# First attention of a transformer layer: value units over three buffers, head outputs with their own, three key buffers, and the first pair's units ahead of one query unit

## The chip, the cores and the metric

The kernel runs on one core of one Trainium2 chip. The metric is the device time of one execution in microseconds (us); lower is better. The core has a matmul engine (TensorE, PE in the profile; PEld is its weight load), a vector engine (DVE), a scalar engine (ACT) and GpSimd (POOL). SyncE (SP) does no arithmetic: it issues all the transfers, one after the other, and an issue that has to wait holds up those behind it. Each engine works through its own list of instructions in the order in which they stand; semaphores make one wait for another.

## What is computed

One layer on 1024 tokens of width 1024, all in float32: a feed-forward block, a token mixer, a second feed-forward block, and norms between them. The token mixer is what the change touches:

```python
h = rmsnorm(x, mix_norm)
proj = h @ w_in                                   # q, k, v of both attentions, gates
# first ("differential") attention, 8 heads, two score maps c = 0, 1 for each head
q, k = rope(q_da), rope(k_da)
p = softmax(causal(q[h, c] @ k[h, c].T / 8))
a = p[c=0] - lam * p[c=1]
y_da[h] = rmsnorm(a @ v_da[h], head_gain[h]) * (1 - lam_init)
# second attention (NSA): 16 query heads over compressed, selected and windowed keys
y_ns = nsa(q_ns, compressed k/v, k_slc, v_slc, k_win, v_win, gates)
out = (sigmoid(g_a) * (y_da @ w_proj_da) + sigmoid(g_b) * (y_ns @ w_proj_nsa)) @ w_out
```

## The kernel before

Every float32 product is made of three matmuls on a high and a low half of each operand: `mm3` writes `hi*hi`, `lo*hi` and `hi*lo` (lines 49 to 51). `split` (line 86) makes the halves: ACT copies the high half, DVE subtracts it for the low half (line 82).

The mixer's projections are cut into *units*, each with one or two weight tiles of 128 columns, and each in two halves `tb` of 512 tokens. Eight times three matmuls (24, on the tensor `gm`) fill one PSUM bank. A *rope unit* (`rope_pair`) has two weight tiles: DVE multiplies `gm` by cosine and sine into the tiles `m13` and `m42`, POOL joins them, `split` writes `rh` and `rl`, and two or three stores take these to DRAM (`sq` queries, `sk` keys of the first attention, `sqn` NSA queries). A *value unit* (`v_da_unit`) has one: DVE scales `gm` into `vt` (a tile with tag `m13`, line 568), PE transposes it (line 571), `split` writes `vh` and `vl` (tags `rh`, `rl`), and two stores take them to `sv`. The pool `mp` that holds `m13`, `m42`, `rh` and `rl` has one buffer for each tag, 4 KB on each partition, so whoever takes a tag next waits until the stores from it have landed.

Before the first attention (`prelim`) come the NSA key, value and query units; each of the four NSA query units `u` is a rope unit with `cmp_block`, scores against the compressed keys. Then `da_phase` runs the query and key unit of head pair 0, and all four units of pair 1 (query, key, value of head 2, value of head 3), with the loads of head 0's two keys and two value halves among them.

After that the eight heads follow each other. For each head and each of four steps `m` there are four query loads (`qt`), and for two rows of tokens `z` and two maps `c` the scores (`S<-kt,qt`, line 789): DVE adds the mask and finds the maximum (line 796), ACT takes the exponential (line 798), then the sums are inverted and the two maps are joined on POOL and DVE (lines 828 to 832). One step later PE transposes the result (line 844), `split` writes `th` and `tl`, and PE multiplies by the values (`o<-th,vt`, lines 866 to 868). Every second step `da_finish2` norms the head's output: it works in the tiles `yr` and `zr`, and then splits the result into two tiles of these same tags, which are stored to `syd`. The remaining units (pairs 2 and 3, then the gates) are *filler*: their matmuls are put between the score steps, one bank at a time.

A head needs two key tiles `kt` (c = 0 and 1) and two value tiles `vt` of 512 KB each. The pool for keys has four buffers (`B_DK`), the one for values two, the one for queries four. Two S tiles are in PSUM at a time.

The program's order is not the one in which it is written: a scheduler in the framework places each engine's instructions by priorities and its own model of their times, once, when the kernel is built. After that the order is fixed.

Of the kernel before, what the change touches and what calls it, by code (L numbers as in the profile page):

```python
# [15 lines left out]
P = 128  # L16
T = 1024
TB = 512
# [56 lines left out]
def drain(units):  # L75
    for u in units:
        for _ in u:
            pass
# [479 lines left out]
            cmp(tb, uh, ul)  # L558


def v_da_unit(K, h):
    nc = K.nc
    w = load_w(K, K.A["win"][C_VDA + h])
    for tb in range(NTB):
        ps = K.gm.tile([P, TB], F32, tag="gm", name="gm")
        yield from fill_gemm(K, ps, w, K.h[tb])
        vt = K.mp.tile([P, TB], F32, tag="m13", name="vt")
        nc.vector.tensor_tensor(out=vt, in0=ps, in1=K.R[tb], op=ALU.mult)
        tr = K.gm.tile([P, 4, P], F32, tag="gm", name="tr")
        for j in range(4):  # L570
            nc.tensor.transpose(tr[:, j], vt[:, j * P:(j + 1) * P], K.ident)
        vh = K.mp.tile([P, 4, P], F32R, tag="rh", name="vh")
        vl = K.mp.tile([P, 4, P], F32R, tag="rl", name="vl")
        split(nc, vh, vl, tr)
        for hl, t in ((0, vh), (1, vl)):
            nc.sync.dma_start(out=K.s_v[h][hl][:, tb * 4:tb * 4 + 4], in_=t.bitcast(F32))
# [303 lines left out]
def da_finish2(K, h, H, ob, sq):  # L880
    nc = K.nc
    tot = K.tr.tile([P, TB], F32, tag="tr", name="tot")
    nc.tensor.matmul(tot, lhsT=K.ones, rhs=sq, start=True, stop=True)
    m = K.op.tile([P, TB], F32, tag="sq", name="m")
    nc.vector.tensor_scalar(out=m, in0=tot, scalar1=1.0 / P, scalar2=EPS, op0=ALU.mult, op1=ALU.add)
    y = K.op.tile([P, TB], F32, tag="yr", name="yr")
    z = K.op.tile([P, TB], F32, tag="zr", name="zr")
    newton_rsqrt(nc, y, z, m, nc.gpsimd)
    nc.vector.scalar_tensor_tensor(out=ob, in0=ob, scalar=K.hgain[:, h:h + 1], in1=y, op0=ALU.mult, op1=ALU.mult)
    yo = [K.op.tile([P, TB], F32R, tag=t, name="yo") for t in ("yr", "zr")]  # L890
    split(nc, yo[0], yo[1], ob)
    for i in range(2):
        nc.sync.dma_start(out=K.s_yda[H][h][:, i], in_=yo[i].bitcast(F32))
# [6 lines left out]
def da_load_parts(K, h):  # L900
    nc = K.nc
    p, s0 = h // 2, (h % 2) * 2
    K.k = []
    for c in range(2):
        t = K.kp.tile([P, T], F32R, tag="k", name="kt")
        nc.sync.dma_start(out=t.bitcast(F32), in_=K.s_k[p][:, :, s0 + c].rearrange("h a d t -> (h a) d t"))
        K.k.append(t)
        yield
    K.v = []
    K.vv[h] = K.v  # L910
    for hl in range(2):
        t = K.vp.tile([P, 8, P], F32R, tag="v", name="vt")
        nc.sync.dma_start(out=t.bitcast(F32), in_=K.s_v[h][hl])
        K.v.append(t)
        yield
# [223 lines left out]
def prelim(K, cg):  # L1139
    nc, A = K.nc, K.A  # L1140
    K.gm = open_pool(K, cg, "gm0", 4, True, side="right")
    with ExitStack() as ctx:
        c0 = open_pool(K, ctx, "pc", 1)
        K.mq = open_pool(K, ctx, "mq", 1)
        K.cp = open_pool(K, ctx, "cp", 2)
        K.tr = open_pool(K, ctx, "tr0", 2, True)
        K.sc = open_pool(K, ctx, "sc0", 2, True)
        K.cmask = c0.tile([P, 8, NC], F32, name="cmask")
        K.rowv = c0.tile([P, 8], F32, name="rowv")
        K.pos = c0.tile([P, 2, 16], F32, name="pos")  # L1150
        K.cw2k = c0.tile([P, 2, 2, P], F32, name="cw2k")
        K.cw2v = c0.tile([P, 2, 64], F32, name="cw2v")
        for t, n in ((K.cmask, "cmask"), (K.rowv, "rowv"), (K.pos, "pos"), (K.cw2k, "cw2k"), (K.cw2v, "cw2v")):
            nc.sync.dma_start(out=t, in_=A[n])
        lp = c0.tile([P, 4, 64], F32, name="lp")
        nc.sync.dma_start(out=lp, in_=A["lam"].partition_broadcast(P))
        pr = c0.tile([P, 2, 64], F32, name="pr")
        nc.vector.tensor_tensor(out=pr, in0=lp[:, 0::2], in1=lp[:, 1::2], op=ALU.mult)
        sm = c0.tile([P, 2], F32, name="lsm")
        nc.vector.tensor_reduce(out=sm, in_=pr, axis=AX.X, op=ALU.add)  # L1160
        nc.scalar.activation(out=sm, in_=sm, func=AF.Exp)
        nc.vector.memset(K.lam, 1.0)
        nc.vector.tensor_tensor(out=K.lam[:, 1:2], in0=sm[:, 1:2], in1=sm[:, 0:1], op=ALU.subtract)
        nc.vector.tensor_scalar(out=K.lam[:, 1:2], in0=K.lam[:, 1:2], scalar1=-LAM_INIT, scalar2=None, op0=ALU.add)
        K.kbh = c0.tile([P, 2, 2, 4, NC], F32R, name="kbh")
        K.kbl = c0.tile([P, 2, 2, 4, NC], F32R, name="kbl")
        K.Gc = c0.tile([P, 8, 16], F32, name="Gc")
        nc.vector.memset(K.kbh.bitcast(F32), 0.0)
        nc.vector.memset(K.kbl.bitcast(F32), 0.0)
        for kv in range(2):  # L1170
            drain([raw_unit(K, kv, None if kv else K.w0)])
        drain([g_unit(K)])
        with ExitStack() as c2:
            K.cz = open_pool(K, c2, "cz", 1)
            K.bt = [None] * 2
            compress_load(K, 0)
            drain([v_ns_unit(K, 0)])
            compress_half(K, 0, 0)
            drain([v_ns_unit(K, 1)])
            compress_half(K, 0, 1)  # L1180
            compress_fin(K, 0)
            compress_load(K, 1)
            drain([rope_pair(K, C_KV, K.s_kv)])
            compress_half(K, 1, 0)
            drain([v_da_unit(K, 0)])
            compress_half(K, 1, 1)
            compress_fin(K, 1)
            drain([v_da_unit(K, 1)])
        for u in range(4):
            drain([rope_pair(K, C_QNS + 2 * u, K.s_qns[u], lambda tb, uh, ul, u=u: cmp_block(K, u, tb, uh, ul))])  # L1190


def da_units(K, p):
    return [lambda: rope_pair(K, C_QDA + 2 * p, K.s_q[p]), lambda: rope_pair(K, C_KDA + 2 * p, K.s_k[p]),
            lambda: v_da_unit(K, 2 * p), lambda: v_da_unit(K, 2 * p + 1)]
# [8 lines left out]

B_W = 2
B_ST = 2
B_DK = 4
B_DV = 2
B_DQ = 4
B_DP = 7  # L1210
# [12 lines left out]
def da_phase(K, cg):  # L1223
    nc = K.nc
    with ExitStack() as ctx:
        K.kp, K.vp, K.qp = open_pool(K, ctx, "dk", B_DK), open_pool(K, ctx, "dv", B_DV), open_pool(K, ctx, "dq", B_DQ)
        K.nk, K.vv = {}, {}
        for n, f in enumerate(da_units(K, 0)[:2] + da_units(K, 1)):
            if n == 2:
                early = da_load_parts(K, 0)  # L1230
            if n >= 2:
                next(early)
            if n == 5:
                q0 = da_queries(K, 0, 0)
            drain([f()])
        cg.close()
        K.low = LOW_DA
        log_exp(K)
# [151 lines left out]
def body(tc, A, out):  # L1390
    nc = tc.nc
    K = Ctx()
    K.tc, K.nc, K.A = tc, nc, A
    K.low, K.vv, K.gate, K.fill, K.seen = 0, {}, None, None, {}
    K.h, K.acc, K.R = [None] * 2, [None] * 2, [None] * 2
    with ExitStack() as ctx:
# [172 lines left out]
```

## Time and profile before

| | us |
|---|---|
| median of 3 timed runs | 2980.08 (2974.42 to 2980.65) |
| the profiled execution | 2971.48 |
| its span in the profile | 2969.7 |
| PE busy | 2860.9 (96% of the span) |
| DVE, ACT, POOL busy | 1981.6, 1268.5, 971.5 |
| mean granted TensorE clock | 0.992 of full speed |

The first attention runs from about 960 us to 1490 us. Times are counted from the start of the span. In a row of the timeline, brackets at the end say how long the engine had been idle before this instruction and what ended that; rows of PE whose matmuls overlap show durations longer than the distance from one to the next. A granted clock of 1.00 is 2.4 GHz, 0.50 is 1.2 GHz, and a number between is a mean over the stretch.

### The profile page before, as it was taken

How to read it: one execution, taken by the hardware profiler on the slowest of the kernel's cores; microseconds unless marked ns; L12 is line 12 of the kernel's file. 1: busy time of each engine (PE TensorE's matmuls, PEld its weight loads, DVE VectorE, ACT ScalarE, POOL GpSimd, SP SyncE). 2: the span in 40 equal slices, each digit the busy share in tenths (PEclk: the TensorE clock that was granted, in tenths of full speed). 3: DMA queues.
4: the chain of work that ended last, by engine and by line, in shares of the span. 5: the costliest groups of instructions: out<-in, count | busy, mean ns of one | idle time of the engine just before them, and what ended most of it. 6: DMA issues, size and time to landing. Idle time of an engine off the chain costs nothing.

```text
span 2969.7 us, 39965 instructions
## 1 busy us (share of the span) xinstructions
PE 2860.9 (96%) x14238; PEld 2390.4 (80%) x14238; DVE 1981.6 (67%) x3140; ACT 1268.5 (43%) x2195; POOL 971.5 (33%) x765
## 2 busy tenths in 40 slices
PE   8999999999999899989899999999999999999998
PEld 6887887888788678778778888888878888788886
DVE  8765666666687467667677777776333866667656
ACT  6322234443233245445566666666432522223443
POOL 4356651000144123222333233333242435664101
PEclk9999999999999999999999999999999999999999
DMA  4345458655456544544332234222742245455854
GB/s 139 113 167 195 155 188 309 215 182 167 153 201 219 185 163 158 180 166 163 113 119 84 86 114 162 77 83 78 290 153 93 71 145 177 164 190 203 290 182 148
DMA packets 212710, 478.19 MB, mean 161 GB/s; under 512 B 20896, under 2 KB 39584, under 8 KB 212512
## 3 DMA queue, kind: packets, MB, share of 16 engines
q1 hardware_dynamic: 212512, 475.65, 46.5%
q8 instruction: 112, 1.84, 0.2%
q14 instruction: 86, 0.70, 0.1%
HBM read 313.56 MB, written 162.00 MB: 160 GB/s over the span
## 4 chain that ended last, share of the span: by engine, by line
PE 67%; DMA 10%; DVE 6%; issue 4%; ACT 3%; POOL 2%; SPq 1%; DVEq 0%; ACTq 0%; POOLq 0%
PE gm L49 6%; PE S L789 6%; PE gm L50 6%; PE gm L51 6%; PE Y L324 5%; PE acc L49 5%; PE acc L51 5%; PE acc L50 5%; PE tr L844 4%; PE Z L324 4%; PE X L324 3%; PE o L1002 2%; PE o L1001 2%; DMA sg<-smx 2%; DVE wlo L82 1%
## 5 line engine op out<-in xcount | busy, mean ns | idle before, releaser
L49 PE MATMUL gm<-hi,whi 128*128 128x512 f32 x880 | 351.3, 399 | 4.1 <-ACT whi L86 1.7
L51 PE MATMUL gm<-hi,wlo 128*128 128x512 f32 x880 | 347.7, 396 | 1.0 <-DVE wlo L82 1.0
L50 PE MATMUL gm<-lo,whi 128*128 128x512 f32 x880 | 348.0, 395 | 0.0
L789 PE MATMUL S<-kt,qt 128*128 128x320 f32 (+5 forms) x1152 | 275.3, 353 | 35.9 <-ACT Pt L798 11.3
L82 DVE TENSOR_TENSOR tl<-tr,th 128x512 fp32r<-128x512 f32 (+2 forms) x384 | 236.2, 619 | 88.1 <-ACT th L86 84.5
L86 ACT ACTIVATE th<-tr 128x512 fp32r<-128x512 f32 (+2 forms) x384 | 203.7, 542 | 197.4 <-PE tr L844 193.8
L82 DVE TENSOR_TENSOR wlo<-st,whi 128x1024 fp32r<-128x1024 f32 x154 | 198.7, 1308 | 116.9 <-ACT whi L86 116.1
L324 PE MATMUL Y<-tf,whi 128*128 128x512 f32 x864 | 269.9, 394 | 4.4 <-DVE c L367 1.8
L796 DVE CUSTOM_DVE_ANT_0 S<-S,slab 128x896 f32<-128x896 f32 (+7 forms) x320 | 224.5, 709 | 65.5 <-PE S L789 59.8
L49 PE MATMUL acc<-whi 128*128 128x512 f32 (+1 forms) x628 | 242.8, 387 | 3.8 <-DVE u L398 3.8
L50 PE MATMUL acc<-wlo,whi 128*128 128x512 f32 (+1 forms) x628 | 242.8, 387 | 0.0
L51 PE MATMUL acc<-whi,wlo 128*128 128x512 f32 (+1 forms) x628 | 242.7, 388 | 0.0
L86 ACT ACTIVATE whi<-st 128x1024 fp32r<-128x1024 f32 x154 | 160.3, 1057 | 192.4 <-PE acc L51 109.7
L955 POOL TENSOR_SCALAR Ps<-Ps,l 128x384 f32<-128x384 f32 (+7 forms) x128 | 100.8, 788 | 426.0 <-DVE l L953 212.6
L789 PEld LDWEIGHTS S<-kt,qt 128*128 128x128 f32 x1152 | 183.5, 190 | 60.7 <-ACT Pw L798 13.2
L82 DVE TENSOR_TENSOR wlo<-a,whi 128x1024 fp32r<-128x1024 f32 x90 | 136.6, 1522 | 96.4 <-ACT whi L86 96.3
L49 PEld LDWEIGHTS gm<-hi,whi 128*128 128x128 f32 x880 | 168.0, 191 | 37.1 <-issue 2.0
L51 PEld LDWEIGHTS gm<-hi,wlo 128*128 128x128 f32 x880 | 167.7, 191 | 37.5 <-DVE wlo L82 1.7
L324 PEld LDWEIGHTS Y<-tf,whi 128*128 128x128 f32 x864 | 161.3, 188 | 45.0 <-issue 4.2
L50 PEld LDWEIGHTS gm<-lo,whi 128*128 128x128 f32 x880 | 167.8, 191 | 30.8
L324 PE MATMUL Y<-tf,wlo 128*128 128x512 f32 x432 | 169.4, 393 | 0.0
L1001 PE MATMUL o<-th,vt 128*128 128x256 f32 (+1 forms) x608 | 164.4, 287 | 1.8 <-ACT th L86 1.7
(314 smaller groups left out, 7007.5 us busy)
## 6 DMA issues: line engine op xcount, KB each, us to landing
wst<-in_win_dram SPq DMA_DIRECT2D x55, 512.0 KB
sw<-w2s SPq DMA_DIRECT2D x44, 512.0 KB
st<-sw SPq DMA_DIRECT2D x88, 256.0 KB
st<-saT SPq DMA_DIRECT2D x88, 256.0 KB
a<-in_f1w_dram SPq DMA_DIRECT2D x36, 512.0 KB
a<-in_f2w_dram SPq DMA_DIRECT2D x36, 512.0 KB
st<-saB SPq DMA_DIRECT2D x66, 256.0 KB
qt<-sq SPq DMA_DIRECT2D x128, 128.0 KB
```

The source lines that it names most:

```text
L49: first = nc.tensor.matmul(out, lhsT=w[0][:, wk], rhs=x[0], start=start, stop=False, skip_group_check=skip)
L50: nc.tensor.matmul(out, lhsT=w[0][:, wk], rhs=x[1], start=False, stop=False, skip_group_check=skip)
L51: nc.tensor.matmul(out, lhsT=w[1][:, wk], rhs=x[0], start=False, stop=stop, skip_group_check=skip)
L82: return nc.vector.tensor_tensor(out=lo, in0=src, in1=hi.bitcast(F32), op=ALU.subtract)
L86: nc.scalar.activation(out=hi, in_=src, func=AF.Copy)
L324: K.mark = nc.tensor.matmul(o, lhsT=w[a][:, m * h + k], rhs=x[k][b], start=start and k == 0 and i == 0, stop=k == h - 1 and i == 2, skip_g ...
L789: K.last = nc.tensor.matmul(S[:, o:o + n], lhsT=q, rhs=k[:, k0 + c:k0 + c + n], start=i == 0, stop=i == 1)
L796: nc.vector.tensor_tensor_reduce(out=sv, in0=sv, in1=mv, scale=-0.125, scalar=BIG, op0=ALU.add, op1=ALU.min, accum_out=nm)
L844: nc.tensor.transpose(tr[:, b * P:(b + 1) * P], src, K.ident)
L955: nc.gpsimd.tensor_scalar(out=p[:, 0:n], in0=p[:, 0:n], scalar1=l[:, c:c + 1], scalar2=1.0, op0=ALU.mult, op1=ALU.mult)
L1001: nc.tensor.matmul(dst, lhsT=v, rhs=hi[:, b * P:(b + n) * P], start=False, stop=False, skip_group_check=True)
L1002: nc.tensor.matmul(dst, lhsT=v, rhs=lo[:, b * P:(b + n) * P], start=False, stop=last, skip_group_check=True)
```

## The change

Four things change.

1. A value unit takes one tile of 4 KB for both halves, `vhl`, and its tag goes round over `m42`, `rh` and `rl`: a counter `vturn` is raised for every half `tb`, and its remainder by three picks the tag.
2. The two output tiles of `da_finish2` get tags of their own, `yh` and `yl`, 2 KB each.
3. The pool of keys has three buffers.
4. The query and key unit of pair 0 run in `prelim`, ahead of the last NSA query unit (`u == 3`). In `da_phase` only pair 1's four units are left; one of head 0's loads stands ahead of each, and its first query loads behind them.

```diff
--- before.py
+++ after.py
@@ -558,6 +558,10 @@
             cmp(tb, uh, ul)
 
 
+def halves(t):
+    return t[:, 0], t[:, 1]
+
+
 def v_da_unit(K, h):
     nc = K.nc
     w = load_w(K, K.A["win"][C_VDA + h])
@@ -569,8 +573,8 @@
         tr = K.gm.tile([P, 4, P], F32, tag="gm", name="tr")
         for j in range(4):
             nc.tensor.transpose(tr[:, j], vt[:, j * P:(j + 1) * P], K.ident)
-        vh = K.mp.tile([P, 4, P], F32R, tag="rh", name="vh")
-        vl = K.mp.tile([P, 4, P], F32R, tag="rl", name="vl")
+        K.vturn += 1
+        vh, vl = halves(K.mp.tile([P, 2, 4, P], F32R, tag=("m42", "rh", "rl")[K.vturn % 3], name="vhl"))
         split(nc, vh, vl, tr)
         for hl, t in ((0, vh), (1, vl)):
             nc.sync.dma_start(out=K.s_v[h][hl][:, tb * 4:tb * 4 + 4], in_=t.bitcast(F32))
@@ -887,7 +891,7 @@
     z = K.op.tile([P, TB], F32, tag="zr", name="zr")
     newton_rsqrt(nc, y, z, m, nc.gpsimd)
     nc.vector.scalar_tensor_tensor(out=ob, in0=ob, scalar=K.hgain[:, h:h + 1], in1=y, op0=ALU.mult, op1=ALU.mult)
-    yo = [K.op.tile([P, TB], F32R, tag=t, name="yo") for t in ("yr", "zr")]
+    yo = [K.op.tile([P, TB], F32R, tag=t, name="yo") for t in ("yh", "yl")]
     split(nc, yo[0], yo[1], ob)
     for i in range(2):
         nc.sync.dma_start(out=K.s_yda[H][h][:, i], in_=yo[i].bitcast(F32))
@@ -1187,6 +1191,8 @@
             compress_fin(K, 1)
             drain([v_da_unit(K, 1)])
         for u in range(4):
+            if u == 3:
+                drain([f() for f in da_units(K, 0)[:2]])
             drain([rope_pair(K, C_QNS + 2 * u, K.s_qns[u], lambda tb, uh, ul, u=u: cmp_block(K, u, tb, uh, ul))])
 
 
@@ -1204,7 +1210,7 @@
 
 B_W = 2
 B_ST = 2
-B_DK = 4
+B_DK = 3
 B_DV = 2
 B_DQ = 4
 B_DP = 7
@@ -1225,14 +1231,11 @@
     with ExitStack() as ctx:
         K.kp, K.vp, K.qp = open_pool(K, ctx, "dk", B_DK), open_pool(K, ctx, "dv", B_DV), open_pool(K, ctx, "dq", B_DQ)
         K.nk, K.vv = {}, {}
-        for n, f in enumerate(da_units(K, 0)[:2] + da_units(K, 1)):
-            if n == 2:
-                early = da_load_parts(K, 0)
-            if n >= 2:
-                next(early)
-            if n == 5:
-                q0 = da_queries(K, 0, 0)
+        early = da_load_parts(K, 0)
+        for f in da_units(K, 1):
+            next(early)
             drain([f()])
+        q0 = da_queries(K, 0, 0)
         cg.close()
         K.low = LOW_DA
         log_exp(K)
@@ -1391,6 +1394,7 @@
     nc = tc.nc
     K = Ctx()
     K.tc, K.nc, K.A = tc, nc, A
+    K.vturn = 0
     K.low, K.vv, K.gate, K.fill, K.seen = 0, {}, None, None, {}
     K.h, K.acc, K.R = [None] * 2, [None] * 2, [None] * 2
     with ExitStack() as ctx:
```

The same instructions are in both programs; from the last NSA query units to the end of the first attention they stand in another order on all engines.

SyncE at the start of the first attention, before (`sk0` is the key scratch of heads 0 and 1, `sq1` the query scratch of pair 1; the four `kt` are the keys of heads 0 and 1):

```order
L553 DMA sk0_76<-rh_7769 128x2x512
L553 DMA sk0_76<-rl_7770 128x2x512
L906 DMA kt_7775<-sk0_76 128x1x1024
L906 DMA kt_7919<-sk0_76 128x1x1024
L906 DMA kt_8761<-sk0_76 128x1x1024
L906 DMA kt_8763<-sk0_76 128x1x1024
L553 DMA sq1_73<-rh_7847 128x2x512 x2
L553 DMA sq1_73<-rl_7848 128x2x512
```

and in the change:

```order
L812 DMA qt_8221<-sq0_72 128x1x256
L784 DMA spc7_0_121<-pp_7612 128x1024
L812 DMA qt_8221<-sq0_72 128x1x256
L812 DMA qt_8224<-sq0_72 128x1x256 x2
L812 DMA qt_8345<-sq0_72 128x1x256 x2
L910 DMA kt_7771<-sk0_76 128x1x1024
L910 DMA kt_7915<-sk0_76 128x1x1024
L812 DMA qt_8348<-sq0_72 128x1x256
L553 DMA sq1_73<-rh_7843 128x2x512 x2
L105 DMA wst_8059<-in_win_dram 128x1024
L553 DMA sq1_73<-rl_7844 128x2x512
L812 DMA qt_8348<-sq0_72 128x1x256
```

The key stores of pair 0 stood directly ahead of the key loads. Now the last of them stands 15 rows ahead of the first key load, with the last NSA query unit's stores between, and only three keys are loaded here.

SyncE where head 7's keys are loaded, before (`sk3` is the key scratch of heads 6 and 7):

```order
L642 DMA smx0_3_126<-vt_11520 128x512
L893 DMA syd1_4_151<-yo_11355 128x512
L893 DMA syd1_4_151<-yo_11356 128x512
L808 DMA qt_11781<-sq3_75 128x1x256 x2
L808 DMA qt_11784<-sq3_75 128x1x256 x2
L906 DMA kt_12144<-sk3_79 128x1x1024
L906 DMA kt_12146<-sk3_79 128x1x1024
L642 DMA smx1_3_134<-vt_11634 128x512
L1055 DMA wst_11683<-in_win_dram 128x1024
```

and in the change, where head 7's first key (`kt_12128`) is loaded 17 rows ahead of this one:

```order
L646 DMA smx1_4_135<-vt_11897 128x512
L1059 DMA wst_11914<-in_win_dram 128x1024
L917 DMA vt_11625<-sv6_0_97 128x1024
L917 DMA vt_11627<-sv6_1_98 128x1024
L812 DMA qt_12136<-sq3_75 128x1x256 x2
L812 DMA qt_12139<-sq3_75 128x1x256 x2
L646 DMA smx0_5_128<-vt_12014 128x512
L910 DMA kt_12130<-sk3_79 128x1x1024
L812 DMA qt_12275<-sq3_75 128x1x256 x2
L897 DMA syd1_5_152<-yo_11849 128x512
L812 DMA qt_12278<-sq3_75 128x1x256 x2
```

The second key of head 7 no longer stands beside the first but behind the loads of the step's queries, since its buffer is the one that head 6's first key had.

ACT around the first half of head 7's value unit, before (`vh`; `Pt` are exponentials, `th` the halves for the value matmuls):

```order
L86 ACTIVATE th_10697<-tr_10692 128x512
L86 ACTIVATE yo_10546<-ob_10428 128x512
L798 ACTIVATE Pt_10670,l_10662<-S_10671,nm_10663 128x256
L86 ACTIVATE th_10712<-tr_10707 128x512
L86 ACTIVATE vh_10479<-tr_10474 128x512
L798 ACTIVATE Pt_10765,l_10763<-S_10766,nm_10764 128x384
L86 ACTIVATE th_10727<-tr_10722 128x512
L798 ACTIVATE Pt_10771,l_10763<-S_10772,nm_10764 128x384
```

and in the change (`vhl`, turn 15 of the counter, so tag `m42`):

```order
L802 ACTIVATE Pt_10479,l_10477<-S_10480,nm_10478 128x1024
L802 ACTIVATE Pt_10487,l_10477<-S_10488,nm_10478 128x1024
L86 ACTIVATE th_10542<-tr_10537 128x512
L86 ACTIVATE vhl_10465<-tr_10460 128x512
L117 ACTIVATE yr_10522<-m_10520 128x512
L802 ACTIVATE Pt_10611,l_10609<-S_10612,nm_10610 128x128
L802 ACTIVATE Pt_10617,l_10609<-S_10618,nm_10610 128x128
L86 ACTIVATE th_10557<-tr_10552 128x512
```

The unit stands somewhat earlier among the scores; what stands behind it on ACT, exponentials and `th`, is of the same kind.

## Rows read from the trace of the kernel before

**Rows 1.** First part of the page: busy time by engine, share, instructions.
```profile
PE 2860.9 (96%) x14238; PEld 2390.4 (80%) x14238; DVE 1981.6 (67%) x3140; ACT 1268.5 (43%) x2195; POOL 971.5 (33%) x765
```

**Rows 2.** Windows: stretch, length, busy PE, PEld, DVE, ACT, POOL, clock, DMA share, GB/s.
```profile
800.00:900.00 100.00, 100.00 (x528) 85.86 (x527) 83.34 (x121) 32.16 (x39) 44.98 (x34) 1.00 0.49 176
...
960.00:1000.00 40.00, 33.12 (x135) 26.76 (x134) 11.02 (x19) 5.04 (x8) 5.48 (x6) 0.87 0.51 167
...
1200.00:1300.00 100.00, 87.73 (x442) 73.77 (x443) 65.97 (x138) 46.73 (x99) 23.36 (x24) 0.92 0.49 175
...
sum 530.00, PE 484.09 PEld 406.84 DVE 348.75 ACT 239.69 POOL 134.53; mean PE 80.68 PEld 67.81 DVE 58.12 ACT 39.95 POOL 22.42
```

**Rows 3.** Waits of PE, 960 to 1490 us: total us, times, longest.
```profile
PE o L866 <- ACT th L86: 6.9, 3, 4.1
PE tr L571 <- DVE vt L568: 4.8, 2, 2.6
...
PE o L866 <- DMA vt<-sv: 2.8, 1, 2.8
```

**Rows 4.** Timeline of PE at its longest idle times: start, duration, instruction.
```profile
980.75 0.45 PE L789 MATMUL S<-kt,qt 128*128 128x128 f32 x1 [3.29 <-issue]
...
985.86 0.66 PE L789 MATMUL S<-kt,qt 128*128 128x128 f32 x2 [3.59 <-DMA kt<-sk]
...
1201.52 0.39 PE L866 MATMUL o<-th,vt 128*128 128x256 f32 x1 [4.10 <-ACT th L86]
...
1249.61 1.56 PE L789 MATMUL S<-kt,qt 128*128 128x512 f32 x4 [2.47 <-ACT Pt L798]
...
1279.18 1.22 PE L789 MATMUL S<-kt,qt 128*128 128x512 f32 x2 [4.59 <-ACT Pt L798]
...
1297.71 0.36 PE L866 MATMUL o<-th,vt 128*128 128x256 f32 x1 [2.79 <-DMA vt<-sv]
...
1476.30 0.58 PE L866 MATMUL o<-th,vt 128*128 128x256 f32 x1 [2.52 <-ACT th L86]
```

**Rows 5.** Windows of 5 and 10 us around these idle times.
```profile
965.00:975.00 10.00, 10.00 (x46) 8.29 (x45) 3.51 (x4) 2.01 (x2) 2.53 (x2) 1.00 0.48 172
...
985.00:990.00 5.00, 4.14 (x11) 3.40 (x12) 2.02 (x6) 0.46 (x2) 0.37 (x1) 0.50 0.66 260
...
1250.00:1255.00 5.00, 5.00 (x17) 3.94 (x16) 3.20 (x6) 3.39 (x7) 1.01 (x1) 0.66 0.47 171
...
1280.00:1285.00 5.00, 5.00 (x18) 4.29 (x18) 2.78 (x8) 1.69 (x5) 0.58 (x1) 0.56 0.31 118
...
1300.00:1305.00 5.00, 5.00 (x21) 3.99 (x20) 1.93 (x2) 0.00 (x0) 3.81 (x4) 0.86 0.56 161
```

**Rows 6.** Timeline of SP: issues of transfers.
```profile
972.73 2.41 SPq L906 DMA_DIRECT2D kt<-sk  x4
...
1239.95 0.38 SPq L553 DMA_DIRECT2D sk<-rh  x1
...
1265.09 1.39 SPq L576 DMA_DIRECT2D sv<-vh  x1
...
1289.97 1.07 SPq L913 DMA_DIRECT2D vt<-sv  x2
```

**Rows 7.** Timeline of ACT where it waited for stores, and one row of DVE.
```profile
1247.97 0.60 ACT L86 ACTIVATE vh<-tr 128x512 fp32r<-128x512 f32 x1 [3.57 <-DMA sk<-rh]
...
1277.97 0.60 ACT L86 ACTIVATE vh<-tr 128x512 fp32r<-128x512 f32 x1 [4.54 <-DMA sv<-vh]
...
1472.38 0.69 DVE L885 TENSOR_SCALAR m<-tot 128x512 f32<-128x512 f32 x1 [4.44 <-PE tot L883]
...
1475.13 0.63 ACT L117 ACTIVATE yr<-m 128x512 f32<-128x512 f32 x1 [8.14 <-DMA syd<-yo]
```

**Rows 8.** Timeline of PE at the change from head 6 to head 7.
```profile
1413.70 2.08 PE L789 MATMUL S<-kt,qt 128*128 128x512 f32 x8
...
1421.33 0.44 PE L789 MATMUL S<-kt,qt 128*128 128x128 f32 x2 [1.25 <-ACT Pt L798]
```

## The prediction, made before the change was run

> **What bounds the kernel now.** I read the first part of the page first: PE is busy for 96% of the span [rows 1], so elsewhere a change can only win or lose what PE waits. Then the windows over the first attention, 960 to 1490 us: PE is busy for 484.1 of 530 us, so 45.9 us are idle, and the granted clock falls below 1 in just those stretches, to 0.87 in the first 40 us and 0.92 after 1200 us [rows 2]. The timeline of PE says where: two waits at the very start, for the first scores and for a key (3.29 and 3.59 us), and later 4.10, 2.47, 4.59, 2.79 and 2.52 us [rows 4]. Each longer wait is paid twice: after it PE runs for some microseconds at a lower clock, 0.50 after the first pair [rows 5]. ACT's and SP's timelines say what ended them: most of these waits are stores or loads that come late, while ACT, which works in order, holds back the exponentials behind a tile that is not free [rows 6, 7]. So the sum is made of single waits of PE. What a lower clock costs I take from the one window behind each wait: busy time times the missing share of the clock.
>
> **First pair's units ahead of a query unit.** No work is added; ten stores and four weight loads move on SP ahead of the last query unit's own, into a stretch where PE was busy for 100.00 of 100 us [rows 2] and four banks lie between it and DVE, so I price the move itself at nothing. Four key loads, for heads 0 and 1, are issued together at 972.73 us, right behind the key stores [rows 6]; the first scores start at 980.75 us, those on the second key at 985.86 us, 13.1 us after [rows 4]. In the change the last of these stores is a whole NSA query unit and pair 1's query unit ahead of the first score, over 190 matmuls; 46 of them touch 10 us at full clock [rows 5], so over 40 us lie between. Both waits go: 3.29 + 3.59 us, and the clock behind them, 0.50 x 4.14 = 2.07 us [rows 5]: 9.0 us. The row of the first does not name its cause; if it is another, 3.29 us less. What is late next: the scores of head 0's first step now stand only 22 matmuls ahead of the first value unit's transposes, so they share ACT and DVE with that unit. There PE waits 4.8 us today, in two pieces, for the value unit's first step on DVE [rows 3]; that unit's first half now takes `rl` instead of `rh` and still waits for a key store. I leave these 4.8 us as they are; they may go, or double.
>
> **Value units over three buffers.** By the counter, pair 1's halves take `rl`, `m42`, `rh`, `rl`, pair 2's `m42`, `rh`, `rl`, `m42`, pair 3's `rh`, `rl`, `m42`, `rh`. ACT's longest wait for the half before is at head 7's unit: its `vh` waited 4.54 us, until 1277.97 us [rows 7], for a store issued at 1265.09 us [rows 6], and PE waited 4.59 us for the exponential behind it [rows 4]. This half now has `m42`, last used by head 5's unit. That wait goes, with 0.44 x 5.00 = 2.2 us of clock [rows 5]: 6.8 us. Head 6's first half still has `rh`, whose key store was issued at 1239.95 us [rows 6] and freed it at 1247.97 us, 8.0 us later [rows 7]; PE waited 2.47 us and lost 0.34 x 5.00 = 1.7 us [rows 4, 5]. In the new order 18 filler matmuls, some 4 us, and a score step stand on PE between this unit's transposes and the first matmul that needs ACT behind it; but the unit also follows its key unit sooner on ACT. All 4.2 us may go, or 2 more may come; I take half, 2.1 us. A new wait comes in: pair 3's query unit writes `m42` on DVE after head 5's unit has stored from it. Behind that write stand the masks of the next scores. Between the two stands one bank of filler and a score step, about 7.5 us; a store takes 8.0 us (above) or 12.9 us (1265.09 to 1277.97), so 0.5 to 5.4 us; I take 0.5, from the store with no burst ahead of it.
>
> **Output tiles of their own.** At 1475.13 us ACT's `yr` ended a wait of 8.14 us for a store from the former output, though its input from DVE was ready at 1472.38 + 0.69 = 1473.07 us [rows 7]. Behind it stood the `th` for which PE waited 2.52 us [rows 4]. 2.06 us of it go: 2.1 us. Elsewhere such a wait does not show on PE: nothing.
>
> **Order of head 4.** Its value loads were issued at 1289.97 us [rows 6], and PE waited 2.79 us for the first, until 1297.71 us [rows 4]. Counted along PE's order, with 0.22 us for a matmul of 512 columns and in proportion below, 3.9 us of work stood between the last use of the old tile and the first of the new. In the change 9.2 us do, as at the other heads, where 8.8 us and more were enough for this to be the stage's only such wait [rows 3]. 2.79 us and 0.14 x 5.00 = 0.7 us of clock [rows 5]: 3.5 us. The 4.10 us at 1201.52 us [rows 4], behind a weight tile that stands behind three stores, keep that neighbour: nothing.
>
> **Three key buffers.** Now a head's second key can be loaded only when the former head's last score on its first key is done. SP waits there, with a query load of the next step behind it. By the same count PE has until the first score on the new key, for heads 1 to 7: 13.5, 9.7, 8.4, 7.5, 6.3, 5.3, 5.0 us (before: 45 to 73). At head 7 these are 4 score matmuls, 12 of filler, 12 on values and 2 of the first key; the order there is the old one, and the trace shows 1413.70 + 1.0 to 1421.33 us, 6.6 us, as the first map's exponential is awaited too [rows 8]. How long one key takes no row shows. The nearest is head 4's value tile, of the same size: 3.9 us of work and 2.79 us of wait, 6.7 us. The ends: nothing, if it takes 5.0 us; 13.1 us, from 972.73 to 985.86 us, the second key with four loads at once [rows 4, 6], would add up to 36.4 us. With 6.7 us heads 5 and 6 wait 0.4 and 1.4, head 7 0.1: 1.9 us.
>
> The Trainium skill, page "SBUF — State Buffer", section "The DMA setup-cost knee", gives a load about 2 us and its bytes at 436 GB/s; estimated from it, a key of 512 KB takes 3.2 us, no head would wait, and the time would come out 1.9 us lower. Here the value tile took 7.7 us from issue to use, on shared queues; the row decides.
>
> **The sum.** Gone: 9.0 + 6.8 + 2.1 + 2.1 + 3.5 = 23.5 us. Added: 1.9 + 0.5 = 2.4 us. The waits of rows 4 but for 1201.52 us make 19.25 us, so 26.7 of the 45.9 idle us are not touched by name; from the last query units on the order is dealt anew on all engines, and these may change by 10 us either way. I add 4 us for this, since a stage that runs closer leaves less slack for stores and loads. 23.5 - 2.4 - 4 = 17.1 us. The profiled execution takes 2971.5 us, 1.8 us around its span of 2969.7, and would take 2954.4 us. The runs' median is 2980.1 us, 8.6 above the profile; so I predict 2963 us.
>
> **Rivals.**
> 1. The waits move. The start is gained, but the new order brings back as many waits as the buffers took away: 9.0 us gained and some 5 us lost, 2976 us. For it: 26.7 us of idle time that no buffer explains. Against it: the units and their buffers, not the order alone, made the longest waits.
> 2. More goes: also the other half at head 6, the 4.10 us and the 4.8 us of rows 3, and nothing comes back: 17.1 + 4 + 2.1 + 4.1 + 4.8 = 32 us, 2948 us. Against it: the buffers these waits turn on are as before.
> 3. Slower, by the keys alone. If a second key takes 11 us, midway between the 8.8 us that suffice for values and 13.1 us, heads 1 to 7 wait 0, 1.3, 2.6, 3.5, 4.7, 5.7 and 6.0 us, 23.8 us in all, and five waits of this length cost some 2 us of clock each: 34 us against 19 gained, 2995 us. It decides from about 9.2 us on, where waits and clock use up the gain. For it: the four loads at the start, and SP's list with up to three stores ahead of a load. Against it: only one value load was awaited, and SP waits for the release, so the queues can empty meanwhile. The Trainium skill, "Trainium Kernel Development and Optimization", section "Best Practices", asks for double buffers to lay transfers beside work; three for two keys keep this for the first key and give it up for the second, which is this rival.
> 4. The start is not cleared: the first wait has another cause, or head 0's queries and keys come late behind the query unit's stores. Then 9.0 us stay: 2972 us. Against it: the 40 us above.
>
> **How the numbers follow.** Chances: the forecast 0.50, waits move 0.20, more goes 0.10, slower by the keys 0.13, start not cleared 0.07. The forecast's own range is 2951 to 2974 us: 10 us either way for the new order and some 2 for the key. The range for 8 in 10 reaches to rival 2 below and past rival 1 above, 2947 to 2985 us. A measurement of this kernel cannot tell less than 0.2%, 6 us, from no change: 2974 and 2986 are the bounds. Faster: nearly all of the forecast, all of "more", a third of "move" and of "not cleared", 0.67. Same: 0.20. Slower: 0.13.
>
> **What would show it.** In the changed profile the first scores start with no wait for a key, and the clock stays at 1.00 between 960 and 1000 us. `vhl` of head 7 has no wait on ACT; head 6's may. No `yr` waits for `syd`. At changes of head PE waits for `kt`, under 2 us each, most at heads 5 to 7. I am wrong if PE waits for keys by over 10 us in all, if the value units' waits on ACT stay, or if idle time of PE in the stage is not below about 35 us.

## The result: slower by 0.73%, and the profile after

| | before | after |
|---|---|---|
| median of 4 runs, us | 2979.82 (2974.42 to 2980.65) | 2997.97 (2992.03 to 2999.06) |
| the profiled execution, its span, us | 2971.48, 2969.7 | 2999.06, 2997.3 |
| mean granted clock | 0.992 | 0.985 |

The ratio on record is 1.0073, 95% interval 1.006 to 1.0086: 18 to 26 us slower. The two medians alone differ by 18 us, 0.61%, which is the lower end of that. The forecast was 2963 us, faster, with a range up to 2985.

The page's first part for the changed kernel, to set beside [rows 1]:

```profile
PE 2871.5 (96%) x14238; PEld 2400.2 (80%) x14238; DVE 1987.5 (66%) x3140; ACT 1269.9 (42%) x2195; POOL 972.7 (32%) x765
```

PE has the same instructions and is busy 10.6 us longer, so they ran slower, as the clock says; the rest of the 27.6 us between the spans is idle time. Some 3 us of them are there already at 708 us (the same weight load is issued at 707.98 us before and at 711.14 us now), ahead of where the two orders part.

The windows of the first attention (columns as in [rows 2]):

```profile
960.00:1000.00 40.00, 40.00 (x197) 33.77 (x196) 19.51 (x31) 8.62 (x12) 13.18 (x10) 1.00 0.63 212
1000.00:1100.00 100.00, 84.28 (x394) 69.42 (x393) 60.86 (x120) 34.77 (x70) 24.00 (x23) 0.91 0.49 174
1100.00:1200.00 100.00, 93.10 (x488) 79.10 (x487) 70.16 (x139) 49.22 (x99) 27.01 (x26) 0.97 0.49 168
1200.00:1300.00 100.00, 85.94 (x446) 72.58 (x445) 66.39 (x138) 44.38 (x92) 28.76 (x27) 0.93 0.44 153
1300.00:1400.00 100.00, 85.61 (x432) 72.18 (x431) 62.91 (x132) 47.48 (x99) 21.67 (x23) 0.92 0.47 158
1400.00:1490.00 90.00, 85.92 (x475) 74.52 (x473) 67.65 (x147) 47.88 (x100) 26.32 (x27) 0.98 0.42 141
sum 530.00, PE 474.85 PEld 401.57 DVE 347.49 ACT 232.36 POOL 140.94; mean PE 79.14 PEld 66.93 DVE 57.91 ACT 38.73 POOL 23.49
```

The first row is as forecast: 40.00 of 40 us and clock 1.00 where before had 33.12 and 0.87 [rows 2]. After it most is worse (not the last row, where before has 80.69 and 0.94): the sum falls from 484.09 to 474.85, and the clock is at 0.91 to 0.93 in three stretches, where before has 1.00, 0.92 and 0.98. PE's timeline at its longest waits in the changed kernel (in brackets the idle time before the instruction, and what ended it):

```profile
1018.99 0.80 PE L793 MATMUL S<-kt,qt 128*128 128x256 f32 x2 [4.86 <-ACT Pt L802]
...
1024.35 0.80 PE L793 MATMUL S<-kt,qt 128*128 128x256 f32 x2 [4.57 <-ACT Pt L802]
...
1176.48 0.80 PE L49 MATMUL gm<-hi,whi 128*128 128x512 f32 x1 [5.87 <-DVE m L544]
...
1282.17 0.66 PE L793 MATMUL S<-kt,qt 128*128 128x128 f32 x2 [7.55 <-DMA kt<-sk]
...
1324.13 0.55 PE L870 MATMUL o<-th,vt 128*128 128x256 f32 x1 [7.09 <-DMA vt<-sv]
...
1397.59 0.66 PE L793 MATMUL S<-kt,qt 128*128 128x128 f32 x2 [4.20 <-DMA kt<-sk]
...
1445.34 0.66 PE L793 MATMUL S<-kt,qt 128*128 128x128 f32 x2 [4.08 <-DMA kt<-sk]
```

Of the waits of [rows 4], those at 980.75, 985.86, 1201.52 and 1476.30 us and head 7's 4.59 us have no successor here. In their place stand: two waits for an exponential in head 0 (9.4 us); 5.87 us behind a write to `m42`; three for second keys, of heads 4, 6 and 7 (15.8 us); and 7.09 us for head 4's values, where before had 2.79. What each hangs on is read from the other engines. ACT's timeline of the changed kernel first:

```profile
1013.17 1.06 ACT L86 ACTIVATE rh<-m 128x1024 fp32r<-128x1024 f32 x1 [13.05 <-DMA sq<-rh]
...
1018.48 0.37 ACT L802 ACTIVATE Pt<-S,nm 128x128 f32<-128x128 f32 x1 [3.30 <-DVE nm L800]
```

At 1013.17 us ACT had waited 13.05 us for the store of pair 1's queries, issued at 998.97 us; this `rh` is the first of pair 1's key unit. The exponential at 1018.48 us waited for DVE, where the maximum of head 0's scores stands behind that unit's `rl` and four of its products:

```profile
1014.44 1.22 DVE L82 TENSOR_TENSOR rl<-m,rh 128x1024 fp32r<-128x1024 f32 x1 [8.29 <-DMA sq<-rl]
...
1018.10 0.29 DVE L800 CUSTOM_DVE_ANT_0 S<-S,slab 128x128 f32<-128x128 f32 x1
```

The maximum for the next score, at 1023.46 us, stands behind the second half's `rl` in the same way. A late store of queries is not new. Before has this row on ACT:

```profile
1000.49 1.06 ACT L86 ACTIVATE rh<-m 128x1024 fp32r<-128x1024 f32 x1 [13.08 <-DMA sq<-rh]
```

But there it is one wait, head 0's first scores were through by 990 us, and PE, with its next work at hand, waited 0.2 us at most between 986 and 1013 us. In the change there are two, 15.90 and 13.05 us, and the first scores stand behind the second. DVE's timeline at the `m42` wait:

```profile
1175.73 0.69 DVE L544 TENSOR_TENSOR m<-gm,sR 128x512 f32<-128x512 f32 x1 [6.75 <-DMA sv<-vhl]
```

The write to `m42` waited 6.75 us for a store of values. Then SP around head 4's second key, the awaited load being the row at 1266.45:

```profile
1264.81 0.53 SPq L926 DMA_DIRECT2D kt<-skv  x1
1265.43 0.45 SPq L580 DMA_DIRECT2D sv<-vhl  x1
1265.94 0.42 SPq L1059 DMA_DIRECT2D wst<-in_win_dram  x1
1266.45 0.53 SPq L910 DMA_DIRECT2D kt<-sk  x1
1267.04 13.06 SPq L812 DMA_DIRECT2D qt<-sq  x4
```

From its issue at 1266.45 us to its use at 1282.17 us this key took 15.7 us. The second keys of heads 6 and 7 are these issues:

```profile
1387.24 0.53 SPq L910 DMA_DIRECT2D kt<-sk  x1
...
1436.07 0.53 SPq L910 DMA_DIRECT2D kt<-sk  x1
```

They took 10.4 and 9.3 us to their use. And the transfers of the whole core while head 4's key was on its way (1270 to 1280 us in 40 slices of 0.25 us: busy share of the 16 DMA engines in tenths, then GB/s; below, one queue's packets, MB and share):

```profile
DMA  8222222222222222222322222123221222212222
GB/s 180 49 49 82 98 98 82 98 98 98 98 115 115 82 98 98 98 115 98 131 82 115 98 115 98 66 82 115 82 115 82 115 115 98 115 82 115 98 115 115
DMA packets 284, 1.00 MB, mean 100 GB/s; under 512 B 24, under 2 KB 24, under 8 KB 284
## 3 DMA queue, kind: packets, MB, share of 16 engines
q1 hardware_dynamic: 284, 1.00, 27.1%
```

Here is what no step of the prediction looked at. In these 10 us, with a key and queries to move and PE waiting for more than half of them, the engines are busy for 27.1% of their time and move 100 GB/s; one stretch of [rows 5] moved 260. A load of a key or of queries takes its 128 rows as `(h a) d t`, and `(h a)` counts 4. A quarter of 16 engines is 4. That these loads run on four engines is read from the two numbers; no row shows one engine by itself.

### The profile page after: what moved, and what is told of

The parts are those of the page before. It is cut to its first block, busy times and chain, and to the rows that moved or that the text cites. A ratio compares the mean times of both kernels' runs of the same rounds, so it can differ in the third digit from the quotient of the medians.

```text
span 2997.3 us, 39950 instructions
## 1 busy us (share of the span) xinstructions
PE 2871.5 (96%) x14238; PEld 2400.2 (80%) x14238; DVE 1987.5 (66%) x3140; ACT 1269.9 (42%) x2195; POOL 972.7 (32%) x765
## 4 chain that ended last, share of the span: by engine, by line
PE 66%; DMA 9%; DVE 7%; issue 4%; POOL 3%; ACT 3%; SPq 1%; DVEq 0%; ACTq 0%; POOLq 0%
PE gm L49 6%; PE gm L51 6%; PE gm L50 6%; PE S L793 6%; PE acc L49 5%; PE acc L51 5%; PE acc L50 5%; PE Y L324 4%; PE tr L848 4%; PE Z L324 3%; PE X L324 2%; PE o L1006 2%; PE o L1005 2%; DVE w2s L431 1%; DVE wlo L82 1%
## 5 line engine op out<-in xcount | busy, mean ns | idle before, releaser
L793 PE MATMUL S<-kt,qt 128*128 128x320 f32 (+5 forms) x1152 | 277.3, 353 | 49.2 <-DMA kt<-sk 15.8
```

The costliest lines, as they stand in the source:

```text
L793: K.last = nc.tensor.matmul(S[:, o:o + n], lhsT=q, rhs=k[:, k0 + c:k0 + c + n], start=i == 0, stop=i == 1)
```

## The experiments

Two theories to begin with. **K**: the key loads are late and make most of the loss. **O**: the order dealt anew makes it. After the first four runs a third, **Q**: the key and query loads keep four DMA engines busy, and whatever else uses these four, every store and weight too, lands late. All ratios are to the kernel before, with 95% intervals; 0.1% is 3 us.

| run | edit | median us | ratio |
|---|---|---|---|
| | the change | 2997.97 | 1.0073 (1.0060 to 1.0086) |
| e1 | before, three keys | 2976.53 | 1.0003 (0.9992 to 1.0014) |
| e5 | before, units moved | 2983.53 | 1.0031 (1.0022 to 1.0041) |
| e6 | before, values rotate | 2972.69 | 0.9992 (0.9983 to 1.0001) |
| e4 | change, four keys, old output tiles | 2984.48 | 1.0032 (1.0021 to 1.0044) |
| e7 | change, no rotation | 2990.04 | 1.0050 (1.0038 to 1.0062) |
| e2 | change, wide loads | 2934.46 | 0.9870 (0.9852 to 0.9888) |
| e3 | before, wide loads | 2929.30 | 0.9848 (0.9834 to 0.9862) |
| e8 | change, all wide | 2919.02 | 0.9815 (0.9802 to 0.9827) |
| e9 | before, all wide | 2922.58 | 0.9837 (0.9823 to 0.9850) |
| e10 | change, all wide, four keys, old output tiles | 2918.82 | 0.9822 (0.9807 to 0.9836) |
| e11 | before, units moved, all wide | 2922.02 | 0.9833 (0.9819 to 0.9848) |
| e12 | before, values rotate, all wide | 2923.83 | 0.9837 (0.9824 to 0.9850) |

**e1, three keys alone.**

```diff
-B_DK = 4
+B_DK = 3
```

> The kernel before with three key buffers and nothing else changed; all engines keep their order through the first attention. Theory K (a second key takes 9 to 16 us from its issue to its use, and that makes most of the loss): PE waits for `kt` at several changes of head, 10 to 25 us in all, the clock drops behind each, and the kernel is 12 to 30 us slower than before. Theory O (the order dealt anew makes the loss, the key waits only stand where another wait would): at most 6 us slower. The forecast's own pricing gives 1.9 us.

Measured: no difference, at most 0.14% slower. The waits of PE for keys, 955 to 1520 us (total, times, longest):

```profile
PE S L789 <- DMA kt<-sk: 8.6, 2, 4.3
```

4.3 of the 8.6 us are the wait at the start, which before has too (3.59 us); the other 4.3 us are head 7's. Theory K falls as it stood: the buffer alone does not cost 12 us. The forecast's 1.9 us lies within the interval, though head 7's wait is 4.3 us where the forecast had 0.1 us.

**e2 and e3, wide loads.** The same edit in the change and in before: the 128 rows are taken d first, so that the outermost dimension counts 32.

```diff
-K.s_k[p][:, :, s0 + c].rearrange("h a d t -> (h a) d t")
+K.s_k[p][:, :, s0 + c].rearrange("h a d t -> d (h a) t")
-K.s_q[p][z:z + 2, ..., m * 256:(m + 1) * 256].rearrange("h a d t -> (h a) d t")
+K.s_q[p][z:z + 2, ..., m * 256:(m + 1) * 256].rearrange("h a d t -> d (h a) t")
```

> The change, with the 128 rows of a key and of a query tile taken in the order d, (h, a) in place of (h, a), d; both operands of a score product are permuted alike, so the sum is the same, and every engine keeps its instructions and their order. In the change DMA runs at a share of 0.2 and about 100 GB/s while keys and queries load, and at 0.9 and up to 400 GB/s in other slices. Theory K with a cause (these loads run on a quarter of the DMA engines, since their outermost dimension counts 4): key loads now move at 300 GB/s and more, PE's waits for `kt` fall from 15.8 us to under 4, and the kernel is 12 to 30 us faster than the change, 2968 to 2986 us. If a key is late because SP issues it late or its buffer is freed late: the waits stay above 10 us and the time within 6 us of the change's. Theory O: the same.

> The kernel before, with the same order of rows in the key and query loads as in the wide loads of the change; every engine keeps its order. Theory K with a cause: the 3.59 us for a key at the start and the 1.8 us for queries near 1396 us go or shrink by half; other waits of before are stores and ACT, so 3 to 12 us faster. If the four-engine loads are not what is late: within 3 us of before.

Both gain far more than was expected: 2.0% on the change (60 us), 1.5% on before, with every engine's list of instructions untouched. Theory O can't explain that. The transfers of the changed kernel with wide loads while head 1's first key and queries load, 975 to 985 us:

```profile
DMA packets 1654, 3.83 MB, mean 383 GB/s; under 512 B 143, under 2 KB 398, under 8 KB 1654
...
q1 hardware_dynamic: 1654, 3.83, 103.5%
```

In the change the same stretch has this:

```profile
DMA packets 751, 1.08 MB, mean 108 GB/s; under 512 B 20, under 2 KB 598, under 8 KB 751
...
q1 hardware_dynamic: 751, 1.08, 30.3%
```

383 GB/s against 108; by the issues there, most of the 383 are stores and weights. And not the keys alone come sooner. ACT's waits for stores of queries in the change, 960 to 1490 us (total, times, longest):

```profile
ACT rh L86 <- DMA sq<-rh: 29.0, 2, 15.9
```

and DVE's:

```profile
DVE rl L82 <- DMA sq<-rl: 27.7, 3, 16.4
...
DVE m L544 <- DMA sv<-vhl: 6.7, 1, 6.7
```

In the change with wide loads ACT has no wait for a store of queries any more, and of DVE's one is left:

```profile
DVE rl L82 <- DMA sq<-rl: 2.4, 1, 2.4
```

These stores write 128 rows in the change and here alike, and nothing but the loads beside them was altered: loads and stores share something. That it is four engines, on which a part of each store stands behind keys and queries, is theory Q; it fits, but no row shows it engine by engine. PE's waits for keys fall from 15.8 to 6.4 us, not under 4 as K expected, and the run is 5 us behind e3 by the medians, with intervals that overlap. What is left is one long wait of PE:

```profile
1242.68 0.66 PE L793 MATMUL S<-kt,qt 128*128 128x128 f32 x2 [6.44 <-DMA kt<-sk]
```

It is head 4's second key again, issued 13.1 us before, and three rows of SP behind a key of the second attention (`kt<-skv`), which in this run is still taken as `(h a) d t`.

**e4, the change with four keys.** The head outputs give up their tiles to make room.

```diff
-B_DK = 3
+B_DK = 4
-    yo = [... for t in ("yh", "yl")]
+    yo = [... for t in ("yr", "zr")]
```

> The change with four key buffers again; to make room the head outputs go back to their former tiles. Order differs from the change's by some 70 rows of PE at one place. Theory K: the 15.8 us for `kt` go, with 4 to 8 us of clock, against some 2 us for the output tiles: 14 to 22 us faster than the change, 2976 to 2984 us, so about as fast as before, the rest of the gain eaten by the new waits at 1014 to 1024 us, at 1171 us and at 1317 us. Theory O: at most 6 us faster than the change.

0.41% or 12 us faster than the change by the ratios (0.32% if each median is set against its own runs of before), a little under what K expected, and no wait for a key is left. So three keys, with the output tiles, do cost in the change's order, where they cost nothing in that of before. 0.32% of loss stay.

**e5 and e6, the units moved alone, the rotation alone.** Their diffs are the hunks of the change at line 1187 and in `da_phase`, and that in `v_da_unit`.

> The kernel before with the first pair's units ahead of the last NSA query unit, and nothing else of the change. The forecast's term for it is -9.0 us, so 2965 to 2970 us. Theory Q (query and key loads keep four of the DMA engines busy for long, and every store and load that also uses these four lands late behind them; the change only moves where this is paid): the two waits at the start go, but the stores of pair 1's query unit land 12 us and more after their issue, and PE waits 6 to 12 us between 1000 and 1030 us; the time stays within 5 us of before.

> The kernel before with only the rotation of the value halves over `m42`, `rh` and `rl`. The forecast's terms for it: -6.8 (head 7), -2.1 (head 6), -3.5 (head 4's values), +0.5 (`m42`): -11.9 us. Theory Q: head 7's wait on ACT goes, but PE waits 5 to 7 us behind pair 3's query unit, whose `m` waits on DVE for a store of values from `m42`, with 2 to 3 us of clock: between 6 us faster and 4 us slower than before.

e5 is 0.31% slower, 9 us, where the forecast had 9.0 us gained. PE's longest wait, in its timeline:

```profile
1009.01 0.80 PE L49 MATMUL gm<-hi,whi 128*128 128x512 f32 x1 [8.58 <-ACT whi L86]
```

and ACT's waits behind it, 960 to 1100 us:

```profile
ACT rh L86 <- DMA sq<-rh: 25.8, 2, 18.0
```

`whi` stands on ACT behind `rh`, and `rh` waits twice for a store of queries, 18.0 us and then 7.8 us; the second stands directly ahead of this `whi`. The wait is what theory Q expected; the time is not, it had said within 5 us. e6 is as fast as before, within 0.2%. Its longest waits of PE, 960 to 1490 us:

```profile
PE o L870 <- DMA vt<-sv: 7.0, 1, 7.0
PE S L793 <- DMA qt<-sq: 6.8, 5, 4.3
```

Head 7's wait of 4.59 us is gone, as forecast, and 6.99 us for head 4's values and 4.26 us for queries stand in its place. The `m42` wait that theory Q named for this run did not come; of the runs with narrow loads, those that rotate and have the units moved too (the change and e4) show it.

**e7, the change without the rotation.**

```diff
-vh, vl = halves(K.mp.tile([P, 2, 4, P], F32R, tag=("m42", "rh", "rl")[K.vturn % 3], name="vhl"))
+vh = K.mp.tile([P, 4, P], F32R, tag="rh", name="vh")
+vl = K.mp.tile([P, 4, P], F32R, tag="rl", name="vl")
```

> The change with the value halves in `rh` and `rl` as before; units moved, three key buffers and own output tiles stay. If the rotation's new wait on `m42` (5.87 us and some clock) is a net loss: 4 to 10 us faster than the change, 2988 to 2994 us. If it saves more at heads 6 and 7 than it costs: 2 to 8 us slower, 3000 to 3006 us. The key waits stay at 10 to 18 us in both.

0.23% or 7 us faster than the change by the ratios, but the intervals overlap, and with each median set against its own runs of before it is 0.11%. With the units moved and three keys the rotation gains nothing and is probably a net loss. The key waits fell too, to 6.1 us (2.71 and 3.39, at heads 6 and 7; head 4's is gone), which neither side expected; the parts do not add up.

**e8 and e9, all wide.** As e2 and e3, and the two `rearrange` of the second attention (`kt<-skv` and `qt<-sqn`) likewise.

> The change with wide loads, and the same order of rows for the second attention's keys and queries too; every engine keeps its order. In the change with wide loads one wait for a key is left, 6.4 us at 1242.7 us, and the load of a second attention's key (`kt<-skv`) stands five issues ahead of the awaited one. Theory Q: it was still that narrow load; the wait falls to under 2 us, the 4.3 us for `qt<-sqn` shrink too, and the time is 6 to 15 us under 2934.5: 2920 to 2929 us. If that key is late because three buffers free it late: the wait stays above 4 us, and the time is 2929 to 2935 us.

> The kernel before with all key and query loads of both attentions wide; every engine keeps the order of before. To be read against the change with the same loads, 2919.0 us. With wide loads in the first attention alone the change was 5 us behind before, and 6.4 us of wait with 4.8 us of clock in 1200 to 1300 us belonged to one key that is gone by now; so without it the rest of the change is worth some 6 us. Theory Q: 2922 to 2928 us here. If nothing is left for the change to gain once the loads are wide: 2916 to 2921 us.

The last key wait goes, as theory Q had it. The transfers of the change, all wide, around head 7's second key (1370 to 1376 us in 40 slices; the last rows: KB of one, and median us from issue to landing):

```profile
DMA  0000000000000099196589979999899999986676
GB/s 0 0 0 0 0 0 0 0 0 0 0 0 0 0 218 137 27 191 82 218 300 382 328 328 410 437 362 341 307 369 273 232 335 389 376 328 246 239 273 225
...
kt<-sk SPq DMA_DIRECT2D x1, 512.0 KB, 4.1
qt<-sq SPq DMA_DIRECT2D x4, 128.0 KB, 3.9
```

The key lands 4.1 us after its issue, with four query loads and an output store behind it; in the change it took 9.3 us to its use, with the same loads behind it. PE's waits in the first attention of the changed kernel come down to this, the longest in total first (960 to 1490 us):

```profile
PE S L793 <- ACT Pt L802: 6.6, 7, 2.0
...
PE S L793 <- DMA qt<-sqn: 1.0, 1, 1.0
```

with this sum of the six windows:

```profile
sum 530.00, PE 515.95 PEld 439.49 DVE 400.10 ACT 278.30 POOL 168.47; mean PE 85.99 PEld 73.25 DVE 66.68 ACT 46.38 POOL 28.08
```

515.95 of 530 us, against 474.85 in the change and 484.09 in before. Before with the same loads (e9) has 515.72: once the loads are wide, the two kernels keep PE busy alike. The change with all loads wide is 2.6% faster than the change, and 1.85% faster than the kernel before: it beats both. Against before with the same loads it is 3.6 us ahead by the medians and 0.22% by the ratios, with intervals that overlap: at most a small gain, which these runs can't tell from nothing. 2922.6 us is the edge of what theory Q expected of it, and 2919.0 us is 1 us below what it expected of e8.

**e10 to e12, the parts again with all loads wide.** Four keys and the old output tiles in the change; the units moved, and the rotation, in before.

> The change, all wide, with four key buffers and the head outputs in their former tiles. Theory Q (three buffers suffice when a key loads fast): the output tiles' wait of some 2 us comes back, 2919 to 2923 us. If three buffers still cost: 2908 to 2916 us.

> The kernel before with the first pair's units moved, all loads wide; the order is that of the run with the units moved alone. There the move cost 9 us, with 8.6 us of wait at 1000 us behind a store of queries. Theory Q: that wait is gone, and so are the two at the start which the move was to remove; within 4 us of before with all loads wide. If the move costs by its order: 5 to 12 us slower than that.

> The kernel before with the value halves rotated, all loads wide. Theory Q: the stores from `rh` and `rl` now land in time, so the rotation has little left to save; 0 to 4 us faster than before with all loads wide. If the stores are slow for another reason: the 9 us for heads 6 and 7 are still there without the rotation, and it gains 6 to 9 us.

Every engine's list in each is that of the same kernel with narrow loads (e4, e5, e6). All three lie within 5 us of e8 and e9, at or near what theory Q expected of each; the rotation is 1.3 us slower than e9 where 0 to 4 us faster was expected. The move that cost 9 us costs nothing now, and the fourth key buffer, worth 12 us together with the tiles, is worth nothing: both were the price of slow transfers, not of the order.

## Why the prediction was wrong

**The loss, part by part.** Three ratios lie on one path: units moved 1.0031 (e5); with the rotation and, as before, four keys and the old output tiles 1.0032 (e4); the whole change 1.0073. So the move costs 9 us, the rotation on top of it nothing, three keys with the output tiles 12 us (the order shifts a little with them). The forecast had -9.0, -11.9 and -0.2 us for these, and +4 for the order.

**The start failed first.** The step was "Both waits go: 3.29 + 3.59 us, and the clock behind them". They did go, and the clock stayed at 1.00 to 1000 us. But the prediction looked for what is late next in the value unit alone, which the first scores share ACT and DVE with, and left "these 4.8 us as they are". What came next was a store: pair 1's query and key units now run while head 0's keys and queries load, ACT waits 15.90 and 13.05 us for `rh` (before once, 13.08 us), and head 0's first scores, which before were through by then, stand on DVE behind the key unit's `rl`. PE pays 9.4 us at 1019 and 1024 us; in e5, with nothing but the move, 8.6 us at 1009 us.

**The key's size.** The step was "The nearest is head 4's value tile, of the same size: 3.9 us of work and 2.79 us of wait, 6.7 us". Equal in bytes, the two are not equal in shape: values are taken by 128 rows, a key by `(h a)` first. Measured in the change were 15.7, 10.4 and 9.3 us, past the 9.2 us from which rival 3 decides, and that rival's 2995 us is the closest number in the prediction. It had the right place and a price of 34 us, and took the start as won; 15.8 us of key waits were measured and some 12 us of time, and the start was lost, so that the number came so near is partly luck. The forecast's own test, "PE waits for keys by over 10 us in all", is met, and idle time of PE in the stage is 55.2 us, not below 35. The upper end of 13.1 us, from the start, was the better row: that load went at the same 100 GB/s. At that rate the 512 KB of one key take 5.2 us by themselves (an estimate), so the shape alone does not make 9 to 16 us; the rest is what shares these engines. For head 4 the second attention's key, issued 1.6 us ahead, is part of it: with that one wide too the last key wait went (e8).

**The rotation.** Head 7's wait went, as written, and `yr` no longer waits for `syd`. The wait on `m42` was priced at 0.5 us, "from the store with no burst ahead of it"; it is 5.87 us, beyond the other end of 5.4. Head 4's values were to come in time; they were awaited 7.09 us. Their buffer was free when the last product on the old tile ended, near 1307.6 us, but four query loads ahead of them on SP took until 1313.68 us, and the values needed 8.3 us more from their issue to their use:

```profile
1305.71 7.97 SPq L812 DMA_DIRECT2D qt<-sq  x4
...
1313.78 1.93 SPq L646 DMA_DIRECT2D smx<-vt  x1
...
1315.81 0.96 SPq L917 DMA_DIRECT2D vt<-sv  x2
```

That is SP's order, which the count of matmuls on PE could not see.

**The cause under all of them.** The prediction took each late transfer as a wait of its own. They share one: the stage's 128 query loads of 128 KB and 16 key loads of 512 KB are 25.2 MB, and at 100 GB/s that is 252 of the stage's 530 us in which four engines are taken (an estimate from the rate above). That each edit moved work closer together and so into that queue is the reading that fits: with wide loads every part comes out near nothing. It was not followed wait by wait. That the rows were readable before is the lesson: the profile of before has the same plateau, 98 to 109 GB/s at a share of 0.2, right behind the four key loads of 972.73 us [rows 6] (965 to 995 us in 40 slices):

```profile
DMA  7999852220002122222222239827934962999798
GB/s 228 382 344 397 332 213 104 98 101 27 0 0 55 60 98 98 98 109 109 109 98 104 104 120 396 325 104 303 412 120 183 404 254 98 213 306 246 180 300 191
```

The Trainium skill, "DMA: Bandwidth & Descriptors", section "Rules for kernel authors", says that an outermost dimension below 16 confines a transfer to at most as many engines as that dimension counts, and to put one outermost that is a multiple of 16. The trace agrees: 27.1% and 100 GB/s with 4 outermost, with 32 outermost head 7's second key lands in 4.1 us, and the median of the stage's sixteen is 5.0 us (e8). The page that the prediction used, "SBUF — State Buffer", gave 3.2 us for a key, an estimate from its formula; that is near the 4.1 us of a wide one, and off by a factor of 3 to 5 for a key as it was loaded among the others.

What stays open: why the rotation is worth nothing alone, and probably costs a few us beside three keys. e7 shows that key waits shrink without it, by 9.7 us; which store or load stood in the way of which key was not taken apart further.

## What to carry to other kernels

Before pricing a transfer by a neighbour of the same size, compare the shapes of their access patterns and look at the DMA share while it runs: here a share near 4 of 16 with work waiting was the mark of loads with 4 outermost, and stores and weights beside them came late. Where a contraction allows it, permute the rows of both operands so that the outermost dimension is large; here that took two lines and was worth 2% of the change and 1.5% of before. Here the edits that moved work closer together paid nothing while the transfers were narrow, so widen first and reorder afterwards: with wide loads none of this change's parts could be told from nothing.

## What the runs showed of the hardware

Loads that use a quarter of the DMA engines' time can make stores late that run beside them. For a store of queries DVE sat idle up to 16.4 us in the change; with nothing altered but the loads beside them the longest is 2.4 us. And the clock follows: the windows at 0.91 to 0.93 in the change are 1.00, 0.95 and 1.00 in e2, and 1.00 in all six windows of e8, without any change in PE's own list.
